# A hybrid attention block: one q/k tile set and one gate moved between fillers, memory weights split further ahead, a longer early output projection

## The chip, the cores and the metric

One core of a Trainium2 chip. The metric is the device time of one execution in microseconds (us). The engines meant below are TensorE (PE; its weight loads PEld overlap its matmuls), VectorE (DVE), ScalarE (ACT), GpSimd (POOL) and SyncE (SP, which issues every DMA of this kernel).

## The reference, cut to what matters

One layer for 512 tokens of width 1024: causal attention (8 heads of 64) and gated linear attention (4 heads) side by side on the same normed input, an output projection, cross-attention into 256 memory tokens, a squared-ReLU MLP, and norms between.

```python
h = rms_norm(x, norm_mix)
qa, ka, va, qg, kg, vg, glr, rg = split(h @ w_in)
o_a = moba_attention(qa, ka, va, rp_table)      # 512 tokens: 2 blocks of 256, both past and own visible: causal softmax
log_a = log_sigmoid(glr @ w_gate_up + b_gate) / 16
o_g = rms_norm(gla_chunked(qg, kg, vg, log_a), g_norm) * silu(rg)
x = x + concat([o_a, o_g]) @ w_out
m = rms_norm(mem, norm_mem)
kx, vx = split(m @ w_xkv)                        # needed by the cross-attention only
...
```

## The kernel before

All activations lie transposed (features on partitions). Every f32 weight tile of 128x1024 is loaded by SP into a staging buffer `wst` (5 of them) and split into two f16 halves in `whl` (10 buffers): ACT writes the high half (L114), DVE the low half (L115). Tiles are numbered in the order of use: `whl16` is the seventeenth. A product then takes three matmul passes for each slice of 128 inputs: high with high, high with low, low with high (L231 to L233 where the weights stand still, L246 to L248 where the activations do). A pass has 512 columns for the token activations and 256 for memory or for half of the tokens.

`W.get(key, look)` makes a tile and the `look` tiles after it at the point in the program where the tile is first used; `LOOK` is 3. PE executes its instructions in the order in which the program writes them. The order on ACT, DVE, POOL and SP is set by a list scheduler when the program is built, and each engine then works strictly through its own list. The rows of order below come from the built programs.

The stretch before the output projection has two parts. In the first, the linear attention (`Gla`, two pairs of heads, pr 0 and 1) is a chain of small matmuls and DVE/ACT steps; a queue of generators, `fill`, puts large products between its steps: `fill(n)` runs n steps of three passes (four to six of 256 columns for memory). The fillers are in order: `vg` (values of the linear attention), `qk_steps(0)`, `qk_steps(1)` (query and key tiles of the causal attention's head pairs: `qk0` and `qk4`, `qk1` and `qk5`), the memory's keys `xk0` to `xk7` and values `xv`, then `qk_steps(2)` (`qk2`, `qk6`) and the gates `rg_steps(0)`, `rg_steps(1)`. Before the first of them stands a transpose of the norm row `wx` on PE (L439).

In the second part, the causal attention works through four head pairs. Pair p needs the tiles of `qk_steps(p)`; `score(qt)` makes two PSUM banks of scores, DVE adds the bias and takes the maximum (L813), ACT the exponential (L817), both write the probabilities as two f16 halves `pq` (ACT L837, DVE L838), SP transposes them by DMA (L844) and `attn_out` (L856, bank `o0` to `o3`) multiplies by the values. Its result is split into `mix0` to `mix3`, one for each pair. The gates go into `mix4` to `mix7`, one for each head of the linear attention: `rg_steps(h)` evicts the product (DVE L415), and then ACT exp, DVE min (L538), ACT log, ACT exp, three DVE steps (L542 to L544), one product with the head's output (L545), and the split (ACT L277, DVE L278) follow one another. Fillers here are the values `va`, `qk_steps(3)` and the gates 2 and 3.

While the last pair's probabilities are on their way, `early_steps` begins the output projection in four PSUM banks `out0` to `out3`, on the slices of `mix` named there (slice k reads `mix`k); `residual_steps` adds the others after `o3`, in two halves of the tokens. The banks for scores, `o` and `out` are five (`sbank`), taken in turn. Everything behind the output projection, from the cross-attention's queries `xq` on, is untouched by the change.

Of the kernel before, what the change touches and what calls it, by code (L numbers as in the profile page):

```python
# [27 lines left out]
LOOK = 3  # L28
LOOK_MLP = 5


# [7 lines left out]
def hybrid_block_kernel(  # L39
# [163 lines left out]
    for n in range(8):  # L203
        W.add(("xv", n), w_xv[n])
    for n in (2, 6, 8, 9):
        W.add(("tt", n), w_tt[n])
    for n in range(4):
        W.add(("va", n), w_vv[n])
    for n in (3, 7, 10, 11):
        W.add(("tt", n), w_tt[n])  # L210
# [13 lines left out]

    def gemm_steps(ps, key, act, c0=0, c1=T, kts=range(8), start=True, stop=True, base=0, **kw):
        wt = W.get(key).rearrange("p s (k c) -> p s k c", k=8)
        kts = list(kts)
        for i, kt in enumerate(kts):
            a = act[base + kt]
            st, sp = start and i == 0, stop and i == len(kts) - 1  # L230
            PE.matmul(ps, wt[:, 0, kt, :], a[:, 0, c0:c1], start=st, stop=False, **kw)  # L231
            PE.matmul(ps, wt[:, 0, kt, :], a[:, 1, c0:c1], start=False, stop=False, **kw)  # L232
            PE.matmul(ps, wt[:, 1, kt, :], a[:, 0, c0:c1], start=False, stop=sp, **kw)  # L233
            yield
# [4 lines left out]

    def gemm_tok_steps(ps, keys, act, t0):  # L240
        ws = [W.get(k).rearrange("p s (k c) -> p s k c", k=2) for k in keys]
        for kt in range(8):
            w = ws[kt // 2]
            a = act[kt]
            st, sp = kt == 0, kt == 7
            PE.matmul(ps, a[:, 0, t0:t0 + P], w[:, 0, kt % 2, :], start=st, stop=False)  # L246
            PE.matmul(ps, a[:, 0, t0:t0 + P], w[:, 1, kt % 2, :], start=False, stop=False)
            PE.matmul(ps, a[:, 1, t0:t0 + P], w[:, 0, kt % 2, :], start=False, stop=sp)  # L248
            yield
# [186 lines left out]
    evict(glr, psg, 1.0)  # L436
    pw_ = sbank("wxt")
    for t in range(4):
        PE.transpose(pw_[:, t * P:t * P + P], wx[:, t * P:t * P + P], ident)  # L439
    DVE.tensor_scalar(wxt, pw_.rearrange("p (n t) -> p n t", t=P)[:, :, 0], SA * IX, None, op0=ALU.mult)  # L440

    def v3(t, s):
        return t.rearrange("p (n t) -> p n t", t=s)

    def vg_steps(t):
        ps = gbank(f"vg{t}")
        yield from gemm_tok_steps(ps, [("vg", j) for j in range(4)], act0, t * P)
        vg[t] = pg.tile([P, 512], F32, name=f"vgs{t}")
        ACT.activation(vg[t], ps, AF.Copy, scale=wxt[:, t:t + 1])
# [67 lines left out]
    def xk_steps(n):  # L517
        ps = gbank(f"xk{n}")[:, :M]
        for i, _ in enumerate(gemm_steps(ps, ("xk", n), actm, c1=M)):
            if i % 2:  # L520
                yield
        kf = pst.tile([P, M], F32, tag="yn", bufs=4, name=f"kf{n}")
        DVE.scalar_tensor_tensor(kf, ps, EM, wm, op0=ALU.mult, op1=ALU.mult)
        split(kx[n][:, 0, :], kx[n][:, 1, :], kf, 1.0)

    def xv_steps(c, t):
        ps = gbank(f"xv{c}{t}")
        yield from gemm_tok_steps(ps, [("xv", 4 * c + j) for j in range(4)], actm, t * P)
        cs = slice(c * 512, c * 512 + 512)
        split(vx[t][:, 0, cs], vx[t][:, 1, cs], ps, wmt[:, t:t + 1])  # L530
# [218 lines left out]
    fill.add(xk_steps(0), xk_steps(1), memrow_steps(), *[xk_steps(n) for n in range(2, 8)])  # L749
    fill.add(*[xv_steps(c, t) for c in range(2) for t in range(2)], qk_steps(2))  # L750
    gl = []
    for pr in range(2):
        fill(5)
        gl.append(Gla(pr))
    for pr in range(2):
        if pr == 1:
            load_bias(0)
        G = gl[pr]
        a = G.prep_fine()
        fill(20 if pr == 0 else 8)  # L760
        G.banks()
        G.small(0, a)
        for i, s in enumerate((8, 16)):
            a = G.prep_level(s)
            fill(5)
            G.small(128 + 128 * i, a)
# [12 lines left out]
        G.outp()  # L779
        fill(8)  # L780
        for hh in range(2):
            G.norm(hh)
            fill(6)
        if pr == 0:
            fill.add(rg_steps(0), rg_steps(1))
    fill.drain()
# [78 lines left out]
    def early_steps():  # L865
        for n in range(NPRE):
            early[n] = sbank(f"out{n}")
            yield from gemm_steps(early[n], ("out", n), mix, 0, T, (0, 1, 4, 5), stop=False, skip_group_check=True)

    def residual_steps(nm, act, hf, ssq):  # L870
        c0 = hf * HT
        for n in range(8):
            if nm == "out" and n < NPRE:
                ps = early[n][:, c0:c0 + HT]
                yield from gemm_steps(ps, (nm, n), act, c0, c0 + HT, (6, 7, 2, 3), start=False, skip_group_check=True)
            else:
# [14 lines left out]
    ssq = sums("out", *HALVES)  # L891
    fill.add(*[va_steps(t) for t in range(4)], qk_steps(3), rg_steps(2), rg_steps(3))
    pairs = {}
    for i in range(5):
        if i < 4:
            pairs[i] = Pair(i)
            if i < 3:
                load_bias(i + 1)
        if i == 3:
            fill.until(2)  # L900
        if i == 4:
# [3 lines left out]
        for g in range(4):  # L905
            if i < 4:
                pairs[i].score(3 - g)
                fill(5)
            elif g > 0:
                fill(4)  # L910
            if 1 <= i < 4 and g == 3:
                fill.until(3)
                attn_out(pairs.pop(i - 1))
        if i < 4:
            pairs[i].trans()
            fill(2)
    fill(4)
    attn_out(pairs.pop(3))
# [493 lines left out]
```

## Time and profile before

| | |
|---|---|
| median of 3 runs | 718.61 us (717.89 to 721.73) |
| profiled execution, its own time | 719.81 us |
| its span (first to last instruction) | 718.0 us |
| mean granted TensorE clock | 0.979 of full speed |
| PE busy | 681.6 us, 95% of the span |
| DVE busy / ACT busy | 553.9 us (77%) / 416.7 us (58%) |

The time is the whole execution as the device counts it, 1.8 us more than the span of the instructions in the same execution. Busy times are unions on one engine; the granted clock is 1.00 at 2.4 GHz and 0.50 at 1.2 GHz. Times within the trace are counted from the span's start.

### The profile page before, as it was taken

What the parts mean: (1) busy time and instruction counts of PE and PEld (TensorE: products, weight loads), DVE (VectorE), ACT (ScalarE), POOL (GpSimd) and SP (SyncE); (2) the same over time, 40 slices, a digit from 0 to 9 for tenths busy, and PEclk for the clock granted to TensorE, in tenths of its full rate; (3) what the DMA queues carried; (4) which work ended last, traced back from release to release, by engine and by line L of the source; (5) the groups of instructions that cost most, each with busy time, mean ns of one, the idle gap of its engine ahead of it and who ended that gap; (6) DMA issues with size and microseconds to landing.
All of it is one profiled execution on the core that took longest, in us unless ns stands there. A gap on an engine that the chain in (4) does not pass through costs nothing.

```text
span 718.0 us, 13472 instructions
## 1 busy us (share of the span) xinstructions
PE 681.6 (95%) x5376; PEld 472.7 (66%) x5376; DVE 553.9 (77%) x987; ACT 416.7 (58%) x800; POOL 72.0 (10%) x90
## 2 busy tenths in 40 slices
PE   8899997999995799999999999999999999999995
PEld 3344574454442378788888854458888866488884
DVE  6899448958888627847639899889888889999825
ACT  7755346846876617456536666555444766665533
POOL 4030010000000024200124100000000000003211
PEclk9999998999999799999999999999999999999998
DMA  8874005752486503325403332203333342314003
GB/s 307 278 259 133 1 1 174 270 174 76 113 236 216 116 21 119 118 60 169 113 16 109 128 102 75 88 31 119 118 119 118 120 164 70 117 50 144 16 1 118
DMA packets 57059, 85.68 MB, mean 119 GB/s; under 512 B 32123, under 2 KB 37540, under 8 KB 56996
## 3 DMA queue, kind: packets, MB, share of 16 engines
q1 hardware_dynamic: 56996, 84.82, 37.4%
q8 instruction: 42, 0.69, 0.4%
q14 instruction: 21, 0.17, 0.1%
HBM read 75.36 MB, written 3.68 MB: 110 GB/s over the span
## 4 chain that ended last, share of the span: by engine, by line
PE 57%; DVE 7%; ACT 2%; issue 2%; POOL 1%; DMA 1%; DVEq 0%; ACTq 0%; POOLq 0%
PE up L232 6%; PE up L233 6%; PE up L231 6%; PE a L1183 4%; PE a L1185 4%; PE a L1184 4%; DVE whl L115 2%; PE xq L231 2%; PE xq L233 2%; PE xq L232 2%; PE c L1184 2%; PE c L1185 2%; PE c L1183 2%; PE out L232 1%; PE out L231 1%
## 5 line engine op out<-in xcount | busy, mean ns | idle before, releaser
L115 DVE SCALAR_TENSOR_TENSOR whl<-wst,whl 128x1024 f16<-128x1024 f32 (+1 forms) x165 | 195.2, 1192 | 26.2 <-ACT whl L114 25.8
L114 ACT ACTIVATE whl<-wst 128x1024 f16<-128x1024 f32 (+1 forms) x165 | 165.6, 1013 | 43.0 <-PE a L1185 8.0
L231 PEld LDWEIGHTS <-whl 128*128 128x128 f16 x752 | 73.9, 98 | 43.3 <-ACT whl L114 5.5
L233 PEld LDWEIGHTS <-whl 128*128 128x128 f16 x752 | 73.9, 98 | 39.9 <-DVE whl L115 1.2
L232 PEld LDWEIGHTS <-whl 128*128 128x128 f16 x752 | 73.9, 98 | 36.2 <-issue 1.6
L232 PE MATMUL up<-act,whl 128*128 128x512 f16 (+1 forms) x224 | 78.1, 349 | 0.0
L233 PE MATMUL up<-act,whl 128*128 128x512 f16 (+1 forms) x224 | 78.1, 349 | 0.0
L231 PE MATMUL up<-act,whl 128*128 128x512 f16 (+1 forms) x224 | 78.1, 349 | 0.0
L1183 PE MATMUL a<-t,whl 128*128 128x256 f16 x192 | 52.3, 273 | 1.1 <-ACT v L1200 1.1
L1185 PE MATMUL a<-t,whl 128*128 128x256 f16 x192 | 52.3, 273 | 0.0
L1184 PE MATMUL a<-t,whl 128*128 128x256 f16 x192 | 52.3, 273 | 0.0
L1184 PEld LDWEIGHTS <-whl 128*128 128x128 f16 x456 | 44.6, 98 | 6.9 <-issue 1.5
L1183 PEld LDWEIGHTS <-whl 128*128 128x128 f16 x456 | 44.6, 98 | 5.2
L1185 PEld LDWEIGHTS <-whl 128*128 128x128 f16 x456 | 44.6, 98 | 5.0
L232 PE MATMUL xq<-act,whl 128*128 128x256 f16 x128 | 34.9, 273 | 0.2 <-DVE act L278 0.2
L233 PE MATMUL xo<-ox,whl 128*128 128x256 f16 x128 | 34.9, 273 | 0.0
L231 PE MATMUL xq<-act,whl 128*128 128x256 f16 x128 | 34.9, 273 | 0.0
L231 PE MATMUL xo<-ox,whl 128*128 128x256 f16 x128 | 34.9, 273 | 0.0
L232 PE MATMUL xo<-ox,whl 128*128 128x256 f16 x128 | 34.9, 273 | 0.0
L233 PE MATMUL xq<-act,whl 128*128 128x256 f16 x128 | 34.9, 273 | 0.0
L277 ACT ACTIVATE t<-hs 128x512 f16<-128x512 f32 x32 | 19.8, 624 | 23.9 <-DVE hs L1065 23.7
L232 PE MATMUL out<-mix,whl 128*128 128x256 f16 (+1 forms) x112 | 32.5, 290 | 0.2 <-DVE mix L278 0.2
(334 smaller groups left out, 1645.2 us busy)
## 6 DMA issues: line engine op xcount, KB each, us to landing
wst<-in_w_up SPq DMA_DIRECT2D x32, 512.0 KB, 3.8
wst<-in_w_down SPq DMA_DIRECT2D x32, 512.0 KB, 4.2
wst<-in_w_tt SPq DMA_DIRECT2D x12, 512.0 KB, 4.6
wst<-in_w_vv SPq DMA_DIRECT2D x8, 512.0 KB, 4.9
wst<-in_w_xk SPq DMA_DIRECT2D x8, 512.0 KB, 4.7
wst<-in_w_xv SPq DMA_DIRECT2D x8, 512.0 KB, 5.2
wst<-in_w_out SPq DMA_DIRECT2D x8, 512.0 KB, 3.7
wst<-in_w_xq SPq DMA_DIRECT2D x8, 512.0 KB, 3.6
```

What stands on the lines that cost most here:

```text
L114: ACT.activation(wt[:, 0, c], stg[:, c], AF.Copy, scale=SW)
L115: DVE.scalar_tensor_tensor(wt[:, 1, c], stg[:, c], SW, wt[:, 0, c], op0=ALU.mult, op1=ALU.subtract)
L231: PE.matmul(ps, wt[:, 0, kt, :], a[:, 0, c0:c1], start=st, stop=False, **kw)
L232: PE.matmul(ps, wt[:, 0, kt, :], a[:, 1, c0:c1], start=False, stop=False, **kw)
L233: PE.matmul(ps, wt[:, 1, kt, :], a[:, 0, c0:c1], start=False, stop=sp, **kw)
L277: ACT.activation(dst_h, src, AF.Copy, scale=scale)
L1183: PE.matmul(ps, w[:, 0, kt, :], b[:, 0, c], start=st, stop=False, skip_group_check=not start)
L1184: PE.matmul(ps, w[:, 0, kt, :], b[:, 1, c], start=False, stop=False, skip_group_check=not start)
L1185: PE.matmul(ps, w[:, 1, kt, :], b[:, 0, c], start=False, stop=sp, skip_group_check=not start)
```

## The change

The transpose of `wx` moves from ahead of the first filler to behind `Gla(0)`'s first matmul (`z0`); the `vg` tiles are made five ahead. The tiles of `xk` and `xv` are made six ahead instead of three. `qk_steps(2)` (48 passes) and `rg_steps(1)` (24 passes) leave the linear attention's fillers and become fillers of the causal attention; the numbers of filler steps are lowered in the first part and raised in the second, and the order of the weight tiles follows. The early output projection takes slices 6 and 7 too, that is, the gates of heads 2 and 3.

```diff
+LOOK_MEM = 6
...
-    for n in (2, 6, 8, 9):
-        W.add(("tt", n), w_tt[n])
+    W.add(("tt", 8), w_tt[8])
     for n in range(4):
         W.add(("va", n), w_vv[n])
-    for n in (3, 7, 10, 11):
+    for n in (2, 6, 3, 7, 9, 10, 11):
         W.add(("tt", n), w_tt[n])
...
-    pw_ = sbank("wxt")
-    for t in range(4):
-        PE.transpose(pw_[:, t * P:t * P + P], wx[:, t * P:t * P + P], ident)
-    DVE.tensor_scalar(wxt, pw_.rearrange("p (n t) -> p n t", t=P)[:, :, 0], SA * IX, None, op0=ALU.mult)
...
-        yield from gemm_tok_steps(ps, [("vg", j) for j in range(4)], act0, t * P)
+        yield from gemm_tok_steps(ps, [("vg", j) for j in range(4)], act0, t * P, 5)
...
-        for i, _ in enumerate(gemm_steps(ps, ("xk", n), actm, c1=M)):
+        for i, _ in enumerate(gemm_steps(ps, ("xk", n), actm, c1=M, look=LOOK_MEM)):
...
-    fill.add(*[xv_steps(c, t) for c in range(2) for t in range(2)], qk_steps(2))
+    fill.add(*[xv_steps(c, t) for c in range(2) for t in range(2)])
...
         gl.append(Gla(pr))
+        if pr == 0:
+            pw_ = sbank("wxt")
+            for t in range(4):
+                PE.transpose(pw_[:, t * P:t * P + P], wx[:, t * P:t * P + P], ident)
...
-        fill(20 if pr == 0 else 8)
+        fill(18 if pr == 0 else 6)
...
-            fill(5)
+            fill(4)
...
-        fill(8)
+        fill(6)
         for hh in range(2):
             G.norm(hh)
-            fill(6)
+            fill(4)
         if pr == 0:
-            fill.add(rg_steps(0), rg_steps(1))
+            fill.add(rg_steps(0))
...
-            yield from gemm_steps(early[n], ("out", n), mix, 0, T, (0, 1, 4, 5), stop=False, skip_group_check=True)
+            yield from gemm_steps(early[n], ("out", n), mix, 0, T, (0, 1, 4, 5, 6, 7), stop=False, skip_group_check=True)
...
-                yield from gemm_steps(ps, (nm, n), act, c0, c0 + HT, (6, 7, 2, 3), start=False, skip_group_check=True)
+                yield from gemm_steps(ps, (nm, n), act, c0, c0 + HT, (2, 3), start=False, skip_group_check=True)
...
-    fill.add(*[va_steps(t) for t in range(4)], qk_steps(3), rg_steps(2), rg_steps(3))
+    fill.add(*[va_steps(t) for t in range(4)], qk_steps(2), qk_steps(3), *[rg_steps(h) for h in (1, 2, 3)])
...
-        if i == 3:
-            fill.until(2)
+        if i in (2, 3):
+            fill.until({2: 4, 3: 3}[i])
...
-                fill(5)
+                fill(5 if i < 3 else 3)
...
-                fill.until(3)
+                fill.until(5)
...
-            fill(2)
-    fill(4)
+            fill(4)
+    fill(6)
```

Three places show how the lists move. The first is ACT's list in the first part, from the first step behind the norm sum `gss1` of pair 0 (`gv1`) on; `whl16` holds the tile of `xk3`, `whl19` that of `xk6`. Before:

```order
L712 ACTIVATE gv1_1166<-gss1_1164,eps_c_85 128x512
L284 ACTIVATE wg1_1169<-gv1_1166 128x512
L581 ACTIVATE qF_1_1230<-dF_1_1228 128x512
L285 ACTIVATE yg1_1168<-wg1_1169 128x512
L277 ACTIVATE kx4_96<-kf4_1188 128x256
L286 ACTIVATE wg1_1169<-yg1_1168 128x512
L582 ACTIVATE kF_1_1231<-dF_1_1228 128x512
L277 ACTIVATE kx5_97<-kf5_1236 128x256
L599 ACTIVATE qz8_1_1340<-d8_1_1338 128x32x8
L600 ACTIVATE kz8_1_1341<-d8_1_1338 128x32x8
L599 ACTIVATE qz16_1_1422<-d16_1_1420 128x16x16
L114 ACTIVATE whl19_1114<-wst19_1113 128x1024
```

and of the change, at the same place:

```order
L707 ACTIVATE gv1_1113<-gss1_1111,eps_c_85 128x512
L284 ACTIVATE wg1_1116<-gv1_1113 128x512
L285 ACTIVATE yg1_1115<-wg1_1116 128x512
L576 ACTIVATE qF_1_1165<-dF_1_1163 128x512
L286 ACTIVATE wg1_1116<-yg1_1115 128x512
L277 ACTIVATE kx2_94<-kf2_1135 128x256
L577 ACTIVATE kF_1_1166<-dF_1_1163 128x512
L594 ACTIVATE qz8_1_1253<-d8_1_1251 128x32x8
L595 ACTIVATE kz8_1_1254<-d8_1_1251 128x32x8
L594 ACTIVATE qz16_1_1329<-d16_1_1327 128x16x16
L115 ACTIVATE whl16_976<-wst16_975 128x1024
L115 ACTIVATE whl17_981<-wst17_980 128x1024
```

The first weight split behind this chain was that of `xk6`; now it is that of `xk3`, three tiles sooner in the order of use. On PE, 36 passes of `xk4` and `xk5` stood between `gss1` and `xk6`; now 12 of `xk2` stand between `gss1` and `xk3`.

The second place is PE's list in the early output projection, behind `out0`'s slices 0, 1 and 4. Before, slice 5 was the last, and `out1` followed:

```order
L231 MATMUL out0_2635<-mix5_110,whl41_2225 128x512
L232 LDWEIGHTS whl41_2225
L232 MATMUL out0_2635<-mix5_110,whl41_2225 128x512
L233 LDWEIGHTS whl41_2225
L233 MATMUL out0_2635<-mix5_110,whl41_2225 128x512
```

and of the change, behind the same slice 5:

```order
L231 MATMUL out0_2635<-mix6_111,whl41_2340 128x512
L232 LDWEIGHTS whl41_2340
L232 MATMUL out0_2635<-mix6_111,whl41_2340 128x512
L233 LDWEIGHTS whl41_2340
L233 MATMUL out0_2635<-mix6_111,whl41_2340 128x512
L231 LDWEIGHTS whl41_2340
L231 MATMUL out0_2635<-mix7_112,whl41_2340 128x512
L232 LDWEIGHTS whl41_2340
L232 MATMUL out0_2635<-mix7_112,whl41_2340 128x512
L233 LDWEIGHTS whl41_2340
L233 MATMUL out0_2635<-mix7_112,whl41_2340 128x512
```

The gates of heads 2 and 3 are now read by the first of the early banks, ahead of `out1`, `out2` and `o3`; before, they were read behind `o3`.

The third place is DVE's list where gate 3 ends (`rge3`, `rgu3`, `rgx3` are its buffers; `whl49` and `whl50` hold tiles of `xq`). Before, its last steps stood ahead of the splits of pair 3's probabilities:

```order
L543 SCALAR_TENSOR_TENSOR rgu3_2489<-rge3_2488,rgu3_2489 128x512
L814 TENSOR_SCALAR sm4_3_2501<-sm4_3_2501 128x2
L544 SCALAR_TENSOR_TENSOR rgx3_2487<-rgx3_2487,rgu3_2489 128x512
L820 RECIPROCAL sm4_3_2501<-sm4_3_2501 128x4
L545 TENSOR_TENSOR rgx3_2487<-rgx3_2487,mix7_112 128x512
L821 TENSOR_SCALAR sm4_3_2501<-sm4_3_2501 128x4
L278 SCALAR_TENSOR_TENSOR mix7_112<-rgx3_2487,mix7_112 128x512
L838 SCALAR_TENSOR_TENSOR pq3_0_2534<-p3_3_0_2510,sm4_3_2501,pq3_0_2534 128x3x128
```

and of the change all of pair 3's splits lie ahead of these rows:

```order
L540 TENSOR_TENSOR rgx2_2505<-rgx2_2505,mix6_111 128x512
L278 SCALAR_TENSOR_TENSOR mix2_107<-o2_2565,mix2_107 128x512
L415 SCALAR_TENSOR_TENSOR rgx3_2605<-rg3_2519,wx_124 128x512
L278 SCALAR_TENSOR_TENSOR mix6_111<-rgx2_2505,mix6_111 128x512
L116 SCALAR_TENSOR_TENSOR whl49_2849<-wst49_2848,whl49_2849 128x1024
L533 TENSOR_SCALAR rge3_2606<-rge3_2606 128x512
L116 SCALAR_TENSOR_TENSOR whl50_2883<-wst50_2882,whl50_2883 128x1024
L537 SCALAR_TENSOR_TENSOR rge3_2606<-rge3_2606,rgu3_2607 128x512
L538 SCALAR_TENSOR_TENSOR rgu3_2607<-rge3_2606,rgu3_2607 128x512
L539 SCALAR_TENSOR_TENSOR rgx3_2605<-rgx3_2605,rgu3_2607 128x512
L540 TENSOR_TENSOR rgx3_2605<-rgx3_2605,mix7_112 128x512
L278 SCALAR_TENSOR_TENSOR mix7_112<-rgx3_2605,mix7_112 128x512
```

Gate 3 has moved behind pair 3's probabilities and behind two weight splits. (The change's line numbers differ by a few from those of before.)

## Rows read from the trace of the kernel before

**Rows 1.** The page: busy us of each engine, share of the span, instructions.

```profile
PE 681.6 (95%) x5376; PEld 472.7 (66%) x5376; DVE 553.9 (77%) x987; ACT 416.7 (58%) x800; POOL 72.0 (10%) x90
```

**Rows 2.** Windows: stretch, length, busy by engine, granted clock, DMA share, GB/s.

```profile
31.45:41.28 9.83, 7.07 (x23) 2.77 (x24) 8.30 (x12) 8.11 (x16) 3.09 (x2) 0.83 0.91 330
...
106.70:120.30 13.60, 7.62 (x49) 5.52 (x48) 11.28 (x19) 7.25 (x11) 0.00 (x0) 0.75 0.35 116
...
224.87:256.65 31.78, 19.66 (x119) 10.19 (x118) 19.96 (x58) 17.37 (x45) 0.00 (x0) 0.79 0.51 125
256.65:287.43 30.78, 30.78 (x280) 27.50 (x280) 17.14 (x33) 15.38 (x31) 12.84 (x14) 1.00 0.23 70
287.43:718.00 430.57, 418.15 (x3356) 326.95 (x3353) 343.40 (x575) 241.49 (x460) 38.51 (x39) 0.99 0.30 95
```

**Rows 3.** Waits of PE: who for whom, us, times, longest.

```profile
PE s L809 <- DVE mix L278: 8.1, 1, 8.1
...
PE o L856 <- DMA pT<-pq: 2.3, 1, 2.3
...
PE s L809 <- DVE sm L813: 1.5, 2, 0.8
...
PE xk L233 <- DVE whl L115: 0.7, 1, 0.7
```

**Rows 4.** Timeline of PE: start, us, instructions, idle before and its releaser.

```profile
34.21 0.66 PE L439 MATMUL wxt<-ident,wx 128*128 128x128 f32 x4 [2.76 <-DVE wx L289]
...
40.43 1.02 PE L557 MATMUL z<-glr,csb 128*128 128x512 f32 x2
...
101.75 1.02 PE L710 MATMUL gss<-gsq,ones 128*128 128x512 f32 x2
...
111.95 0.39 PE L231 MATMUL xk<-mix,whl 128*128 128x256 f16 x1 [5.24 <-ACT whl L114]
...
129.74 0.38 PE L246 MATMUL xv<-whl,mix 128*128 128x512 f16 x1
...
132.76 0.38 PE L248 MATMUL xv<-whl,mix 128*128 128x512 f16 x1
...
171.08 0.82 PE L809 MATMUL s<-qks,qks 64*128 64x512 f16 x6
...
210.48 0.66 PE L809 MATMUL s<-qks,qks 64*128 64x384 f16 x6
...
253.39 1.82 PE L856 MATMUL o<-pT,vas 128*64 128x512 f16 x24
```

**Rows 5.** Timeline of DVE, the same columns.

```profile
34.08 1.22 DVE L115 SCALAR_TENSOR_TENSOR whl<-wst,whl 128x1024 f16<-128x1024 f32 x1
35.21 2.47 DVE L415 SCALAR_TENSOR_TENSOR gqk<-g,wx 128x512 f32<-128x512 f32 x4
37.60 0.68 DVE L415 SCALAR_TENSOR_TENSOR glr<-glr,wx 128x512 f32<-128x512 f32 x1
...
38.27 0.54 DVE L726 COPY bvec<-bv 8x384 f32<-8x384 f32 x1
...
240.87 0.69 DVE L278 SCALAR_TENSOR_TENSOR mix<-rgx,mix 128x512 f16<-128x512 f32 x1 [0.69 <-ACT mix L277]
241.48 2.73 DVE L838 SCALAR_TENSOR_TENSOR pq<-p,sm,pq 128x384 f16<-128x384 f32 x6
...
245.13 1.41 DVE L838 SCALAR_TENSOR_TENSOR pq<-p,sm,pq 128x256 f16<-128x256 f32 x4
```

**Rows 6.** Timeline of ACT, the same columns.

```profile
110.86 3.88 ACT L114 ACTIVATE whl<-wst 128x1024 f16<-128x1024 f32 x4
```

**Rows 7.** Windows, from pair 2's second score to gate 3's split.

```profile
211.14:241.56 30.42, 18.54 (x124) 8.97 (x125) 24.63 (x75) 21.99 (x56) 0.00 (x0) 0.81 0.74 201
```

**Rows 8.** Timeline of SP's DMA issues: x for the residual, pair 2's transposes.

```profile
217.00 5.24 SPq L888 DMA_DIRECT2D xr<-in_x_t  x8
...
231.48 5.27 SPq L844 DMA_TRANSPOSE pT<-pq  x2
```

More of the change, by code (lines that the diff above doesn't have):

```diff
@@ L222, in hybrid_block_kernel, with gemm_steps @@
             W.add_unit(m, j)
-    def gemm_steps(ps, key, act, c0=0, c1=T, kts=range(8), start=True, stop=True, base=0, **kw):
-        wt = W.get(key).rearrange("p s (k c) -> p s k c", k=8)
+    def gemm_steps(ps, key, act, c0=0, c1=T, kts=range(8), start=True, stop=True, base=0, look=LOOK, **kw):
+        wt = W.get(key, look).rearrange("p s (k c) -> p s k c", k=8)
         kts = list(kts)
@@ L238, in gemm, with gemm_tok_steps @@
             pass
-    def gemm_tok_steps(ps, keys, act, t0):
-        ws = [W.get(k).rearrange("p s (k c) -> p s k c", k=2) for k in keys]
+    def gemm_tok_steps(ps, keys, act, t0, look=LOOK):
+        ws = [W.get(k, look).rearrange("p s (k c) -> p s k c", k=2) for k in keys]
         for kt in range(8):
@@ L527, in xv_steps @@
         ps = gbank(f"xv{c}{t}")
-        yield from gemm_tok_steps(ps, [("xv", 4 * c + j) for j in range(4)], actm, t * P)
+        yield from gemm_tok_steps(ps, [("xv", 4 * c + j) for j in range(4)], actm, t * P, LOOK_MEM)
         cs = slice(c * 512, c * 512 + 512)
@@ L754, in hybrid_block_kernel @@
         gl.append(Gla(pr))
+        if pr == 0:
+            pw_ = sbank("wxt")
+            for t in range(4):
+                PE.transpose(pw_[:, t * P:t * P + P], wx[:, t * P:t * P + P], ident)
+            DVE.tensor_scalar(wxt, pw_.rearrange("p (n t) -> p n t", t=P)[:, :, 0], SA * IX, None, op0=ALU.mult)
     for pr in range(2):
```

## The prediction

> **What bounds the kernel now.** I read the page first: TensorE is busy for 681.6 of 718.0 us, so a gain must come out of its idle time or its slow clock [rows 1]. The chain of waits and the windows by stage say where those lie. From 287.43 us on, where `xq` starts, TensorE is busy 418.15 of 430.57 us and nothing is changed there [rows 2]. The loss ahead of that has three places [rows 2 to 4].
>
> - The start: TensorE waits 2.76 us for the norm row before `wxt`, and `z` starts at 40.43; 31.45 to 41.28 runs at 0.83.
> - The memory's keys: 106.70 to 120.30 takes 13.60 us for 48 passes. At full speed a pass of 256 columns takes 30.78 / 280 = 0.110 us; I use 0.114, so 5.5 us would do. The rest is a wait of 5.24 us for ACT's split `whl19`, one of 0.7, and about 2 us of the slower clock (0.75).
> - The attention's tail: 224.87 to 256.65 has 19.66 us busy in 31.78, with waits of 8.1 (a score bank held until DVE has split a `mix`), 2.3 and 1.5 us.
>
> So the sum follows TensorE to the start of `xq`, and asks of every wait who releases it.
>
> **The start.** In the new lists `vg` runs right behind the gate's small product, and `z0` still reads `glr`, which DVE evicts. That eviction starts at 37.60 and `bvec` behind it at 38.27 [rows 5]. One weight split moves from ahead of it to behind it: 35.21 - 34.08 = 1.13 us less. `bvec` moves ahead: its 0.54 row, of which some 0.47 show start to start, more. `glr` then ends near 38.27 - 1.13 + 0.47 = 37.6, `z0` starts near 37.7 instead of 40.43, and the `wxt` transposes behind it take about 0.33 at full clock: 2.4 us saved. The other end: the wait is still about 2 us, and if the clock falls as before, the 9.83 us with 7.07 of work [rows 2] give up to 1.7 back: 0.7 saved. I take 2.4.
>
> **The memory.** Six tiles ahead would remove the 5.24 us if the split could be done earlier. But ACT works through its list in order: after `gss1` (101.75) come pair 0's norm and pair 1's preparation, and only at 110.86 the four splits of 0.97 us each [rows 4, 6]. In the new list the first split behind the same chain is `xk3`'s instead of `xk6`'s. So TensorE's release stays where it is, about 9.1 us behind `gss1`'s start, while its cover shrinks from 36 passes to 12: 24 x 0.114 = 2.7 us more wait, 7.9 instead of 5.24. One split of a key (a few tenths of a us) has left that stretch of ACT's list, so the lower end is 2.4. Afterwards a split comes every 1.13 us and a tile lasts 24 x 0.114 = 2.7 us; the 0.7 wait may go, I leave it. The DMAs are covered: their share there is 0.35 [rows 2].
>
> **Where the attention starts.** The 48 passes of `qk2` and `qk6` and the 24 of gate 1 are now behind it. A pass of 512 columns: 129.74 to 132.76 holds 14 of them, 0.216 us each [rows 4]; 72 x 0.216 = 15.5. The first score moves from 171.08 to 171.08 - 15.5 - 2.4 + 2.7 = 155.9.
>
> **To pair 2's second score.** Before, that ends at 211.14, 40.06 us after the first score, without a wait. Now 15 more passes stand before it (3.2 us), and pair 2's first score must wait for `qk6`, whose last product is just ahead of it. Eviction and split of `qk6` and the weight splits that ACT and DVE have ahead of them, 1.0 and 1.13, with 0.6 to split, are covered by three passes: 2.2 us (1 to 3). So 45.5 us, and the score ends at 201.4.
>
> **To gate 3's split.** From here DVE and ACT set the pace. Before, `mix7` was finished 30.42 us after this score, with DVE busy 24.63 of them [rows 7]. In the new list DVE has more ahead of `mix7`: gate 1's seven steps, each 0.60 start to start as the four `gqk` (2.47 us) show [rows 5], 4.2; the eviction and split of one more tile, 1.2; two weight splits, 2.3; pair 3's probabilities, 2.73 + 1.41 = 4.1; `o2`'s split, 0.6. Together 12.4, so 42.8 us, and `mix7` comes at 155.9 + 45.5 + 42.8 = 244.2, against 241.56 before. Lower end: DVE never waits, 24.63 + 12.4 = 37.0, `mix7` at 238.4. Upper end: it waits in the same proportion, 37.0 x 30.42 / 24.63 = 45.7, 247.1. I take the middle, since the added steps fill some of the 5.8 us but need ACT between them.
>
> On these starts there is a rule against the change. The four `gqk` start 0.60 apart although one lasts 0.68, and the weight splits 1.13 apart against 1.22 [rows 5]. The Trainium skill, "VectorE: DVE Perf Modes", section "The DRAIN you can't avoid", says that the next DVE operation doesn't start until the pipe is empty. By that rule each of some 18 added steps costs about 0.08 us more, 1.4 in all, and the result would be 1.4 us later than mine. The rows say otherwise for instructions that wait for nothing, and the measurement decides.
>
> **TensorE until then and after.** The work left between the second score and `out0`'s gate slices is about 31 us (30 passes of `qk3` and `qk7` and 72 of gates 22.0, six groups of scores at 0.3 to 0.8 together 3, `o1` and `o2` 1.82 each, 12 passes of `out0` 2.6), so TensorE gets there near 232.3 and waits, first for `mix6`, then for `mix7`, 12 us in all. These waits replace the 8.1 and 2.3 of before. After `mix7` follow 2 passes of `out0` and 36 of `out1` and `out2`, 38 x 0.216 = 8.2, and some 2.1 us of clock, as the old tail lost. Then `o3`. From `o3` to `xq` it was 287.43 - 253.39 = 34.0. Slices 6 and 7 of four banks in two halves, 48 passes x 0.110 = 5.3, are gone; `out3`, which stood ahead of `o3`, comes behind it with 18 passes, 3.9. That gives 32.6. So `xq` starts at `mix7` + 42.9 = 287.1 instead of 287.43: **0.3 us saved**.
>
> The transfers don't enter this. SP's eight loads of x (217.00, 5.24 us of issue) stand, in the new list, behind gate 3's last product (near 230) and ahead of pair 3's transposes, which in pair 2 began at 231.48 [rows 8]. Those would land some 8 us behind the loads, near 243; `o3` starts near 254.5. That cover of 11 us hides them; without it the loads would cost up to 5.2.
>
> The profiled execution took 719.81 us, so 719.5 after. The median of the runs is 1.2 us below that execution: **718.3 us**. Half a per cent, 3.6 us, is about what a measurement of this kernel can tell from no change. The break-even is `mix7` at 244.5; faster by 3.6 needs it by 240.9 (a stretch of 39.5 us in place of 42.8), slower by 3.6 from 248.1 on (46.7).
>
> **The rivals.**
> *Fewer waits on DVE.* The fillers lie more evenly now and DVE is the only limit of the stretch: `mix7` at 238.4, `xq` at 281.3, 6.1 us faster, 712.4. For it: five of DVE's 30.42 us were waits that more work can fill. Against it: each gate is a chain through ACT and DVE, and gate 3 now stands last. 0.17.
> *The fillers fill all of the attention's idle time.* TensorE would never wait behind the first scores: `o3` at 232.3 + 9.1 = 241.4, `xq` at 274.0, 13.4 us, 705.2. It needs `mix7` within 31.6 us, less than the 37.0 of work that DVE has by my count. 0.03. The Trainium skill, "Perfetto Trace Analysis", section "Identifying the Most-Contended Engine", says that interleaving regimes with different contended engines may improve performance; this would be that case.
> *The look ahead does remove the memory's wait.* Then the attention starts 7.9 us sooner, and with some 2 us of clock and the 0.7 regained about 11 us are saved: 707.4. Against it: the split's place in ACT's list. 0.04.
> *Slower: gate 3's chain crosses between ACT and DVE behind pair 3's probabilities.* DVE's last rows alternate between gate 3 and two weight splits, with ACT's exponentials and logarithms between. If DVE's waits in the stretch are 12 us instead of 5.8, it is 49 us, `mix7` comes at 250.4, and the kernel takes 724.2. It decides from 46.7 us on, or from 9.7 of waits. For it: the upper proportion already gives 45.7; against it: before, the same gate chain ran within 5.8 us of waits. 0.18.
> That the start saves 0.7 only costs 1.7 and leaves the time within the half per cent: 720.0.
>
> **How the numbers follow.** My forecast, no change to be measured, has 0.58, and its own range is 714.7 to 722.2. Faster: 0.17 + 0.03 + 0.04 = 0.24. Slower: 0.18. The range of 711.8 to 724.0 takes in DVE without waits and most of the slower case, and leaves out the two large gains, some of the slow case, and what I have overlooked.
>
> **What the profile after would show.** Right: `z0` at 37 to 38 behind a wait of about 2 us; one wait of some 8 us on ACT's `whl` at `xk3`; the first score near 156; a wait of about 2 us on `qks` at pair 2's first score; `out0` waiting for `mix6` and `mix7` until about 244, and no long wait for a score bank or for `pT`; `xq` near 287. Wrong: if the wait at `xk3` is short, the attention starts by 150 and the whole gains; if `mix7` is done by 239 or behind 248, DVE's count is wrong, and its busy time between the second score and `mix7` (37 expected) tells whether by work or by waits; if `o3` waits for `pT`, SP's order was the miss.

## The result and the profile after

The changed kernel takes 728.3 us (median of 4 runs, 726.67 to 728.91); the kernel before took 718.25 beside it (717.41 to 721.73). The ratio is 1.0127 (95% interval 1.009 to 1.0164; the two medians alone would give 1.014): slower, where no change was forecast. The profiled execution took 728.34 us, 8.5 more than that of before. The rows below, of its page, show that TensorE's work is about that of before [rows 1]: 24 instructions fewer, since 48 passes of 256 columns became 24 of 512. The 8.6 us of longer span are waits (4.9 us of idle time) and slow clock (3.7 us more busy).

```profile
span 726.6 us, 13422 instructions
PE 685.3 (94%) x5352; PEld 469.6 (65%) x5352; DVE 553.3 (76%) x987; ACT 416.6 (57%) x800; POOL 75.1 (10%) x90
```

The waits of TensorE, who for whom, us, times, longest (against [rows 3]):

```profile
PE out L231 <- ACT mix L277: 8.3, 2, 5.4
PE xk L231 <- ACT whl L115: 7.6, 1, 7.6
PE xq L232 <- DVE act L278: 3.3, 5, 1.1
PE psL L609 <- DVE kF L579: 1.6, 1, 1.6
...
PE z L552 <- DVE glr L415: 1.4, 1, 1.4
...
PE s L809 <- ACT qks L277: 1.0, 1, 1.0
PE s L809 <- DVE qks L278: 1.0, 1, 1.0
...
PE xq L231 <- ACT act L277: 0.9, 2, 0.5
PE out L232 <- DVE mix L278: 0.8, 1, 0.8
```

The long waits for a score bank, for `pT` and for `wx` are gone. The gates' (`out`), the memory's (`xk`) and the two small ones (`z`, `qks`) were forecast. Not forecast are those of `psL` (the small products of the linear attention) and of `xq`. The timeline of TensorE gives the places (against [rows 4]):

```profile
37.35 1.13 PE L552 MATMUL z<-glr,csb 128*128 128x512 f32 x2 [1.40 <-DVE glr L415]
...
56.31 0.76 PE L609 MATMUL psL<-qF,kF 64*32 64x32 f32 x64 [1.64 <-DVE kF L579]
...
105.99 0.40 PE L231 MATMUL xk<-mix,whl 128*128 128x256 f16 x1 [7.63 <-ACT whl L115]
...
158.92 0.82 PE L809 MATMUL s<-qks,qks 64*128 64x512 f16 x6
...
205.45 0.66 PE L809 MATMUL s<-qks,qks 64*128 64x384 f16 x6
...
248.40 0.59 PE L231 MATMUL out<-mix,whl 128*128 128x512 f16 x1 [5.44 <-ACT mix L277]
...
258.76 0.62 PE L856 MATMUL o<-pT,vas 128*64 128x512 f16 x3
...
291.21 0.27 PE L231 MATMUL xq<-act,whl 128*128 128x256 f16 x1
292.36 0.27 PE L232 MATMUL xq<-act,whl 128*128 128x256 f16 x1 [0.89 <-DVE act L278]
```

DVE's timeline has the end of gate 3's split:

```profile
248.38 0.69 DVE L278 SCALAR_TENSOR_TENSOR mix<-rgx,mix 128x512 f16<-128x512 f32 x1 [0.69 <-ACT mix L277]
```

Step by step, in us:

| | before | forecast | after |
|---|---|---|---|
| `z0` starts | 40.43 | 37.7 | 37.35 |
| wait of `xk` on ACT | 5.24 | 7.9 | 7.63 |
| first score | 171.08 | 155.9 | 158.9 |
| from there to pair 2's second score's end | 40.06 | 45.5 | 47.2 |
| from there to the end of `mix7`'s split | 30.42 | 42.8 | 43.0 |
| `o3` starts | 253.39 | 254.5 | 258.76 |
| from `o3` to `xq` | 34.04 | 32.6 | 32.45 |
| from `xq` to the end of the span | 430.57 | 430.57 | 435.4 |

Against the 719.5 us that the prediction had for this execution, it is 8.8 us late: `xq` starts 4.1 us later than forecast, and 4.8 us more go behind it. The windows by stage (length, busy by engine, clock) show where; first those of the changed kernel:

```profile
206.10:248.86 42.76, 33.69 (x204) 14.52 (x203) 37.73 (x95) 30.20 (x69) 0.00 (x0) 0.92 0.60 173
...
291.20:403.90 112.70, 108.50 (x966) 95.33 (x965) 74.90 (x164) 59.11 (x142) 18.65 (x17) 0.98 0.34 93
403.90:726.60 322.70, 312.20 (x2392) 232.51 (x2389) 271.62 (x421) 185.06 (x325) 20.50 (x24) 0.99 0.29 94
```

and the last two stretches in the kernel before:

```profile
287.43:395.10 107.67, 106.12 (x967) 94.46 (x965) 71.88 (x155) 56.45 (x136) 18.04 (x16) 1.00 0.35 98
395.10:718.00 322.90, 312.03 (x2392) 232.49 (x2389) 271.52 (x421) 185.04 (x325) 20.46 (x24) 0.99 0.29 94
```

DVE's 37.73 us busy of the 42.76 (a window that ends 0.2 us short of `mix7`'s split) is near what was counted (37.0 of 42.8). The loss behind `xq` lies wholly in the cross-attention: 112.70 against 107.67 us up to the MLP's first product `up`, and no more behind it. Of these 5.0 us, 2.6 are more idle time (4.20 against 1.55) and 2.4 are longer busy time (108.50 against 106.12): behind the waits TensorE's clock fell, and from 299.8 to 302.8 a pass of 256 columns starts every 0.21 us instead of every 0.11.

### The profile page after: what moved, and what is told of

Read it like the earlier page. It is cut to its first block, busy times and chain, and to the rows that moved or that the text cites. A ratio compares the mean times of both kernels' runs of the same rounds, so it can differ in the third digit from the quotient of the medians.

```text
span 726.6 us, 13422 instructions
## 1 busy us (share of the span) xinstructions
PE 685.3 (94%) x5352; PEld 469.6 (65%) x5352; DVE 553.3 (76%) x987; ACT 416.6 (57%) x800; POOL 75.1 (10%) x90
## 4 chain that ended last, share of the span: by engine, by line
PE 59%; DVE 8%; ACT 3%; issue 1%; POOL 1%; DVEq 0%; ACTq 0%; POOLq 0%
PE up L232 6%; PE up L231 6%; PE up L233 6%; PE a L1183 4%; PE a L1185 4%; PE a L1184 4%; PE xq L232 2%; PE xq L233 2%; PE xq L231 2%; PE c L1184 2%; PE c L1183 2%; PE c L1185 2%; DVE whl L116 2%; PE out L232 1%; PE out L233 1%
## 5 line engine op out<-in xcount | busy, mean ns | idle before, releaser
L232 PE MATMUL xq<-act,whl 128*128 128x256 f16 x128 | 35.5, 277 | 3.3 <-DVE act L278 3.3
L231 PE MATMUL xq<-act,whl 128*128 128x256 f16 x128 | 35.5, 277 | 0.9 <-ACT act L277 0.9
L233 PE MATMUL xq<-act,whl 128*128 128x256 f16 x128 | 35.5, 277 | 0.0
```

## The experiments

All ratios are to the kernel before on the same chip, over 4 to 11 runs of each variant and 11 to 17 of the kernel before; times within a run are those of one profiled execution.

### What each part does by itself

**Six early slices alone**: the kernel before with this edit, and nothing else.

```diff
-            yield from gemm_steps(early[n], ("out", n), mix, 0, T, (0, 1, 4, 5), ...)
+            yield from gemm_steps(early[n], ("out", n), mix, 0, T, (0, 1, 4, 5, 6, 7), ...)
-                yield from gemm_steps(ps, (nm, n), act, c0, c0 + HT, (6, 7, 2, 3), ...)
+                yield from gemm_steps(ps, (nm, n), act, c0, c0 + HT, (2, 3), ...)
```

> The kernel before with one part of the change alone: the early output projection takes slices 6 and 7 (six slices early, two behind o3). Theory A (the early gates cost twice, once in front of o3 and once behind the second half of the residual, where the norm for xq loses its cover): here the gates are on time, since mix7 was finished at 241.6 and out0 reads it near 245, so only the second cost shows: xq starts at 286 to 288, then waits for its input some 4 us in all, and the kernel takes 722 to 724. Rival B (only the lateness of the gates costs, the shorter residual nothing): 717 to 719.

1.0045 (1.0028 to 1.0062), 723.4 us. `xq` starts at 287.1, as before, and then waits:

```profile
PE xq L232 <- DVE act L278: 3.0, 4, 1.0
...
PE xq L231 <- ACT act L277: 0.5, 1, 0.5
```

From `xq` on it takes 435.7 us instead of 430.6. Theory A, not B: with gates on time the six slices still cost 3 us (by the medians).

**The changed kernel with this edit undone** (the same lines the other way; four early slices, and the first two steps of the residual, `out0`'s slices 6 and 7, still stand ahead of `o3`):

> The changed kernel with slices 6 and 7 put back behind o3. Theory A: TensorE reaches out0 at 235, runs 48 passes (10.4 us) without a wait, o3 starts near 246, mix7 (249) is waited for 1 to 2 us at most, xq starts near 281 to 283 and runs without waits: 711 to 715, faster than the kernel before. Rival B (the gates that were moved are late wherever they are read): the 5.4 us wait for mix7 stands behind o3 and the time stays at 722 or more.

0.9929 (0.991 to 0.9949), 715.3 us. `o3` starts at 248.10 instead of 258.76, `xq` at 283.3, and the rest is back at 430.6. Between the profiled executions lie 12.7 us: 1.5 up to the first score (157.4 and 158.9), 9.2 from there to `o3`, 4.8 behind `xq`, less 2.8 between `o3` and `xq`. The 1.5 are not the edit's: up to there the two programs have the same lists on every engine. The edit that looked like a rearrangement of equal work turned a gain into a loss. Rival B is out: read later, the gates are waited for 3.5 us in all instead of 9.1 (1 to 2 were forecast).

**The fillers alone**: the kernel before with the moved tile set, gate and filler numbers; start, look ahead and early slices as before. Against the run above:

```diff
-LOOK_MEM = 6
+LOOK_MEM = 3
...
     evict(glr, psg, 1.0)
+    pw_ = sbank("wxt")
+    for t in range(4):
+        PE.transpose(pw_[:, t * P:t * P + P], wx[:, t * P:t * P + P], ident)
...
-        yield from gemm_tok_steps(ps, [("vg", j) for j in range(4)], act0, t * P, 5)
+        yield from gemm_tok_steps(ps, [("vg", j) for j in range(4)], act0, t * P)
```

> The kernel before with the moved tile set and gate and the numbers of filler steps alone (start, look ahead and early slices as before). Theory A: what the start gained was given back at the first small products of pair 0, and the look ahead only moved the memory's wait, so this stands within 1.5 us of the run with slices 6 and 7 put back: 712 to 716. Rival: start and look ahead are worth 3 us or more together, and this is 3 us or more slower than that run.

0.9895 (0.988 to 0.991), 712.5 us, the best of the parts, and better than the run before it by more than the 1.5 us allowed between them in spans (712.0 against 713.9). The first score comes at 154.5, against 157.4 in that run. So start and look ahead together cost some 2 us. The wait at `xk` is the row below; that of the run with start and look ahead is 7.6, as in the changed kernel:

```profile
PE xk L231 <- ACT whl L115: 4.5, 1, 4.5
```

**The start alone**: the kernel before with the transposes of `wx` behind `z0` and `vg` five ahead.

```diff
         gl.append(Gla(pr))
+        if pr == 0:
+            pw_ = sbank("wxt")
...
-        yield from gemm_tok_steps(ps, [("vg", j) for j in range(4)], act0, t * P)
+        yield from gemm_tok_steps(ps, [("vg", j) for j in range(4)], act0, t * P, 5)
```

> The kernel before with the moved transpose of wx and the vg tiles five ahead alone. Prediction's step: z0 starts 2.4 us or more sooner, and all of it is kept: 715 to 716. Theory A: z0 starts some 3 us sooner, but psL or a later step of pair 0's chain, or the wait at xk, takes it back: 717.5 to 719.

0.9991 (0.9979 to 1.0003), 719.5 us: the prediction's step (715 to 716) is out. `z0` starts at 37.2, 3.2 us sooner, and the first score at 171.4, 0.3 us later. A new wait of `psL` takes 1.9 us of it; the waits at `xk` are 5.5 together, against 5.9, and the rest lies in no single wait:

```profile
PE psL L609 <- DVE kz L597: 1.9, 1, 1.9
```

**Gate 1 left in the linear attention**: the fillers alone, but only `qk2` and `qk6` moved.

```diff
-            fill.add(rg_steps(0))
+            fill.add(rg_steps(0), rg_steps(1))
...
-    fill.add(*[va_steps(t) for t in range(4)], qk_steps(2), qk_steps(3), *[rg_steps(h) for h in (1, 2, 3)])
+    fill.add(*[va_steps(t) for t in range(4)], qk_steps(2), qk_steps(3), *[rg_steps(h) for h in (2, 3)])
```

> The run with the fillers alone, but gate 1 stays in the linear attention; only the tile set qk2, qk6 moves (48 of 72 passes). The attention of before waited 8.1, 2.3 and 1.5 us. If the tile set fills most of that and gate 1's 24 passes (5.2 us) find little left, the ratio is within 0.002 of the 0.9895 of both; if the gate pays as well in proportion, it is 0.992 to 0.995.

0.9888 (0.9862 to 0.9915), 712.3 us, no different from both. In the profiled executions the attention from first score to `xq` takes 120.2 us with the tile set and 126.5 with the gate too: 24 passes, 5.2 us of work, took 6.3 us there. The tile set (10.4 us of work) took 3.9 more than the 116.3 of before [rows 2, 4]. It used up the idle time, and the gate found none.

### Where the time behind xq goes

**Slices 6 and 7 early for the first half of the tokens only**, in the changed kernel:

```diff
-            yield from gemm_steps(early[n], ("out", n), mix, 0, T, (0, 1, 4, 5, 6, 7), ...)
+            yield from gemm_steps(early[n], ("out", n), mix, 0, T, (0, 1, 4, 5), ...)
+            yield from gemm_steps(early[n][:, :HT], ("out", n), mix, 0, HT, (6, 7), start=False, ...)
-                yield from gemm_steps(ps, (nm, n), act, c0, c0 + HT, (2, 3), ...)
+                yield from gemm_steps(ps, (nm, n), act, c0, c0 + HT, (6, 7, 2, 3) if hf else (2, 3), ...)
```

> The changed kernel with slices 6 and 7 early for the first half of the tokens only; the second half adds them behind o3 as before. Theory A: the second half's 24 passes again cover the norm, the waits of xq (4.2 us) fall below 0.5 and the stretch from xq's start to the end is 4 to 5 us shorter than in the changed kernel (435.4); the wait of out0 for the gates stays at 8 us or more, so the ratio to before is 1.003 to 1.008. Rival: xq's waits come from the late gates or from elsewhere, and the stretch stays at 434 or more, the ratio at 1.011 or more.

1.0052 (1.0031 to 1.0072), 722.9 us. The gates are waited for as long as ever, and behind `xq` everything is as before:

```profile
PE out L231 <- ACT mix L277: 8.7, 2, 5.9
PE ssqout L332 <- POOL accout L327: 1.4, 1, 1.4
...
PE xq L232 <- DVE act L278: 0.2, 1, 0.2
```

Theory A, as forecast. The norm of the first half runs while TensorE works on the second half of the residual; 24 passes of that half (2.6 us) had been taken away. In the kernel before and in this run `xq` starts 13.9 us behind the norm's sum `ssqout` (273.57 before); in the changed kernel it is 11.4, by the first row and the start of `xq` above. But the same edit also reordered DVE's list. The second row is the split of the first `act` tile in the changed kernel, the third that of the kernel before:

```profile
279.80 0.60 PE L332 MATMUL ssqout<-accout,ones 128*128 128x256 f32 x2
```

```profile
291.90 0.41 DVE L278 SCALAR_TENSOR_TENSOR act<-ynout,act 128x256 f16<-128x256 f32 x1
```

```profile
283.11 1.08 DVE L278 SCALAR_TENSOR_TENSOR act<-ynout,act 128x256 f16<-128x256 f32 x3
```

It comes 12.1 us behind `ssqout` there and 9.5 before (9.5 in this run too). So this run shows that the 24 passes are the cause, and leaves open how much goes by the shorter cover and how much by the order of the lists. The next two runs ask that.

**Own buffers for the squares**, four instead of the two shared ones, for the residual's second half of the changed kernel. Behind it stands this piece of the changed kernel's ACT timeline, where the norm's square root `yout` lies behind a square that waits for POOL:

```profile
281.31 0.40 ACT L316 ACTIVATE sqout<-xr 128x256 f32<-128x256 f32 x1
283.25 0.42 ACT L316 ACTIVATE sqout<-xr 128x256 f32<-128x256 f32 x1 [1.54 <-POOL accout L327]
283.57 0.40 ACT L285 ACTIVATE yout<-wout 128x256 f32<-128x256 f32 x1
```

```diff
+                if self.name in own:
+                    sq = own[self.name].tile([P, self.n], F32, tag="sqo", bufs=4, ...)
...
+    own[f"out{HT}"] = s4.enter_context(tc.tile_pool(name="psq", bufs=4, reuse_waits="tile"))
```

> The changed kernel with four buffers of their own for the squares of the residual's second half, so that ACT needn't wait there for POOL's sums; the order of ACT's list stays. Theory E, the norm for xq is late because its square root on ACT (yout) stands behind a square that waits 1.5 us for POOL: yout comes 1.5 us sooner behind ssqout, xq's waits fall from 4.2 to about 2.5, the ratio to 1.010 to 1.011. Rival F, only the lost cover counts (24 passes, 2.6 us) and the rest is DVE's list: xq's waits stay at 4 us, the ratio at 1.012 to 1.013.

1.0109 (1.0086 to 1.0131), 727.5 us; this doesn't part E from F. ACT now shows:

```profile
280.19 0.40 ACT L285 ACTIVATE yout<-wout 128x256 f32<-128x256 f32 x1
```

`yout` comes 2.1 us behind `ssqout` (278.1) instead of 3.8 (279.8), but DVE's list puts weight splits (at 283.37 and 285.38) around the two steps that use it, and `xq` still waits 3.3 us.

**The residual's second half in the order `out4` to `out7`, `out0` to `out3`**, in the changed kernel:

```diff
-        for n in range(8):
+        for n in (4, 5, 6, 7, 0, 1, 2, 3) if nm == "out" and hf else range(8):
```

> The changed kernel with the residual's second half in the order out4 to out7, out0 to out3. The passes between ssqout and xq are as few as in the changed kernel, but in ACT's list the norm's three steps now stand ahead of the squares and of all weight splits but one. Theory E (the norm chain is held up in the lists): the first act tile is ready 8 to 9.5 us behind ssqout instead of 12, xq's waits fall below 1 us, 3 to 4 us come back, ratio 1.007 to 1.009. Rival F (lost cover only): xq's waits stay at 3 us or more, ratio 1.011 or more.

1.009 (1.0067 to 1.0112), 726.0 us. DVE splits the first `act` tile 6 us behind `ssqout` instead of 12, and `xq`'s wait falls to 1.0, but the other half's norm waits in its place:

```profile
PE ssqout L332 <- POOL accout L327: 3.0, 1, 3.0
...
PE xq L232 <- DVE act L278: 1.0, 1, 1.0
```

4.0 us in all, nearly as in the changed kernel; 434.5 us from `xq` on. The ratio alone would pass for E, but of the 3.1 us between the profiled spans 2.2 lie ahead of `xq`. E was right on the order and wrong on what it is worth: of the 4.8 us behind `xq`, 0.9 came back. In this run and the changed kernel, with 24 passes fewer, one of the two norms is waited for, whichever comes first.

### What sets the memory's wait

**The changed kernel with four early slices and the start as before**: the fillers alone, but with `LOOK_MEM` 6.

> The changed kernel with slices 6 and 7 behind o3 and the start as before (the wx transpose ahead of the first filler, vg three ahead); the memory's tiles stay six ahead. It stands beside two runs: slices 6 and 7 put back (ratio 0.9929 to before, wait of 7.6 us at the first xk split behind gss1) and the fillers alone (0.9895, 4.5 us). Theory C, the move of the wx transpose makes the memory's wait longer, since in its lists the splits of xk3 to xk5 have moved behind pair 0's norm chain: here they stand ahead of it again, the wait is about 4.5 us and the ratio 0.988 to 0.991. Rival D, the six tiles ahead do it: the wait stays near 7.6 us and the ratio near 0.993.

0.9915 (0.989 to 0.9941), 713.8 us; the wait at `xk` is 4.5 us again. The ratio is just above C's 0.988 to 0.991, but the wait decides for theory C: with these fillers the moved transpose makes it 7.6, and the six tiles ahead change nothing that shows. SP's timeline says how. Before (L731 spreads the bias vector over 1.5 MB of DRAM; six loads of `xk` stand ahead of it, so the first behind it is that of `xk6`):

```profile
39.23 1.07 SPq L113 DMA_DIRECT2D wst<-in_w_xk  x2
...
40.74 0.76 SPq L731 DMA_DIRECT2D bscr<-bscr  x1
48.96 12.61 SPq L113 DMA_DIRECT2D wst<-in_w_xk  x2
```

and in the changed kernel, where three stand ahead of it and the first behind it is that of `xk3`:

```profile
34.73 0.80 SPq L114 DMA_DIRECT2D wst<-in_w_xk  x2
38.92 0.77 SPq L726 DMA_DIRECT2D bscr<-bscr  x1
...
39.78 23.25 SPq L114 DMA_DIRECT2D wst<-in_w_xk  x5
```

With the transposes gone from before `bvec`, the bias goes out earlier, ahead of three more loads. In the programs of before, of the change and of the fillers alone, the first weight split behind pair 0's norm chain is that of the first tile loaded behind this DMA. The start alone fits less well: there too `xk3` is the first load behind the DMA, but its split stands between the norms of pair 0's two heads, and the waits at `xk` came to 5.5 us, not more than before. So the 7.6 us need the moved transpose and the new fillers together.

**That DMA issued by POOL instead of SP**, in the kernel before:

```diff
-    nc.sync.dma_start(
+    nc.gpsimd.dma_start(
         bass.AP(tensor=bscr.tensor, ...),
         bass.AP(tensor=bscr1.tensor, ...),
     )
```

> The kernel before with one DMA moved: the spreading of the bias vector in DRAM (bscr from bscr, 1.5 MB) is issued by POOL instead of SP. In every run so far the first weight split that lies behind pair 0's norm chain is that of the first tile whose load stands behind this DMA on SP: xk6 before (wait 5.2 us), xk3 with the moved wx transpose (7.6 us), xk6 again with the start undone (4.5 us). Theory G, the place of this DMA on SP sets the memory's wait: here the splits lie ahead of the chain, the waits at xk fall below 1 us, the first score moves from 171.1 to 164 to 166, ratio 0.990 to 0.994. Rival H, ACT and DVE have no room and the chain of pair 0 or 1 waits instead: first score at 169 or later, ratio 0.997 or more.

0.9932 (0.991 to 0.9954), 715.3 us. No wait at `xk` is left; the first score starts at 164.5, 6.6 us sooner, and `xq` at 281.0, 6.4 sooner. Theory G.

**The same with the fillers alone:**

> The run with the fillers alone (0.9895) and the same DMA on POOL. Theory G: the waits of 4.5 and 0.7 us at xk go, with some 1 to 2 us of slow clock, first score at 148 to 150 instead of 154.5, ratio 0.981 to 0.984. Rival H: 0.987 or more.

0.9869 (0.9841 to 0.9897), 709.9 us, the lowest ratio here, though its interval overlaps that of the fillers alone. The wait at `xk` is gone, but the first score comes only 1.3 us sooner (153.2). The splits, now early, stand in DVE's list ahead of `kz`; the timelines of DVE and then TensorE:

```profile
58.65 4.60 DVE L116 SCALAR_TENSOR_TENSOR whl<-wst,whl 128x1024 f16<-128x1024 f32 x4
63.17 0.41 DVE L602 TENSOR_TENSOR kz<-kz,gqk 128x256 f32<-128x256 f32 x1
```

```profile
63.73 0.88 PE L614 MATMUL psL<-qz,kz 64*32 64x32 f32 x64 [4.98 <-DVE kz L602]
```

So the place in the list is G's, and most of its gain goes as H said.

**The same with start and six tiles ahead** (four early slices):

> The changed kernel with slices 6 and 7 behind o3 and the same DMA on POOL; the start and the six tiles ahead stay. Theory G with C (the moved transpose cost the memory's wait through SP's order only): the wait of 7.6 us goes too, first score at 147 to 150 instead of 157.4, ratio 0.979 to 0.984, within 1.5 us of the fillers alone with this DMA. Rival D: the wait stays at 4 us or more, ratio 0.988 or more.

0.9917 (0.9887 to 0.9947), 713.9 us, first score at 157.6: a miss. The 7.6 us at `xk` are gone, as C and G have it, but `psL` waits 8.2 us for `kz` and 2.8 for `kF`, and nothing is gained. `kz` stands behind four weight splits in this list too; they take 6.74 us here, 4.60 in the run above.

**The two last runs with the old numbers of filler steps in the linear attention** (20 and 8, 5, 8, 6):

```diff
-        fill(18 if pr == 0 else 6)
+        fill(20 if pr == 0 else 8)
...
-            fill(4)
+            fill(5)
...
-        fill(6)
+        fill(8)
...
-            fill(4)
+            fill(6)
```

First the fillers alone with the DMA on POOL,

> The run with the fillers and the bias DMA on POOL (ratio 0.9869, first score 153.2), with the numbers of filler steps in the linear attention as before (20 and 8, 5, 8, 6 where the change has 18 and 6, 4, 6, 4). There the memory's wait was gone, but TensorE waited 1.2 and 5.0 us at psL of pair 0, for kF and for kz behind four weight splits on DVE (4.6 us), where the kernel before with the same DMA waited 1.9 us. Theory J, the lowered numbers take pair 0's cover away: psL waits 2 us or less in all, first score at 148 to 150, ratio 0.980 to 0.984. Rival K, DVE's chain sets the pace and the fillers used here are missing later: psL or another step of pair 1 waits as much, first score at 152.5 or later, ratio 0.986 or more.

0.9886 (0.9858 to 0.9913), 711.5 us. `psL` waits 1.5 us and the first score starts at 150.6, 2.5 us sooner: so far J. But `xq` starts at 278.6, against 277.6 with the lowered numbers; from first score to `xq` it now takes 128.0 us instead of 124.4. In the result K (the two ratios are not apart), though not by pair 1: the attention gave it back. Then the same with start and six tiles ahead:

> The changed kernel with slices 6 and 7 behind o3, the bias DMA on POOL (0.9917, first score 157.6, psL waits 8.2 and 2.8 us) and the old numbers of filler steps. Theory J: psL's waits fall by 3 us or more, first score at 152 to 154, ratio 0.985 to 0.988. If the moved start pays once its cover is back, it comes within 0.002 of the run without it; if the start is what makes DVE's chain late (e of pair 0 behind the memory's squares on ACT), it stays 2 us or more behind that run.

0.9919 (0.9887 to 0.995), 713.3 us. The wait for `kz` stays at 7.6 us. By the medians the run is 1.8 us behind the last one, but the two intervals overlap, and the run also has six tiles ahead: that the start itself costs time here isn't shown. What it can run into is in ACT's timeline of the changed kernel,

```profile
44.22 0.63 ACT L490 ACTIVATE sqm<-memf 128x512 f32<-128x512 f32 x1 [3.32 <-POOL accm L491]
44.76 1.04 ACT L115 ACTIVATE whl<-wst 128x1024 f16<-128x1024 f32 x1
45.70 0.67 ACT L556 ACTIVATE e<-z,gsb 128x512 f32<-128x512 f32 x1
```

beside the kernel before:

```profile
42.27 0.69 ACT L561 ACTIVATE e<-z,gsb 128x512 f32<-128x512 f32 x1 [0.54 <-DVE g L559]
```

`z0` is ready 3 us sooner, but `e`, the next step, stands behind a square of the memory that waits for POOL, and starts 3.4 us later than before. That belongs to this execution and not to the lists alone: in four other runs whose lists are the same up to the early output projection (four early slices, first half only, own buffers, other order) `e` starts at 42.6, 44.9, 42.5 and 41.9, and with the start alone at 41.3. What differs is POOL's pace (last section).

## Why the prediction was wrong

**"From 287.43 us on nothing is changed there"** is the step that failed: it took 435.4 us and not 430.57, 4.8 of the 8.8 us by which the forecast was missed. The instructions are the same, but `xq` reads the norm of the first half, and the prediction itself took its cover away: it booked the 24 passes of the second half as saved between `o3` and `xq` and didn't ask what ran beside them. The half-only run puts them back and has all of it back (430.6). The term had been right in size (32.6 forecast, 32.45 measured); its other side was missing. In the changed kernel that side was 2.6 us of idle time, as much as the 24 passes take, and the slow clock behind the waits.

**The start, "2.4 us saved"**, was right to `z0` and lost behind it: in the profiled execution at the next step of the chain, ACT's `e`, and at `psL`; with slow clock and smaller waits the first score came 3.0 us later than forecast. In the four other runs with the same lists it came at 157.4 to 158.5, so 1.5 to 2.6 us late whatever `e` did. Alone, the start is worth nothing (0.9991), though `e` starts 1.0 us sooner there.

**The memory's wait** was right in size (7.9 forecast, 7.63) and only half explained. That the new lists put `xk3` behind the norm chain was read off; that, with the new fillers, the moved transpose did it, through a DMA on SP, wasn't. That the six tiles ahead remove nothing was right.

**To pair 2's second score**, 47.2 instead of 45.5: the wait for `qks` was 2.0 us as forecast, but the slow clock (0.96 for the stretch, 1.00 before) was left out.

**The DVE chain to gate 3** was right: 43.0 us, 42.8 forecast. That the two agree to 0.2 us is partly luck, since 0.7 us more work and 0.8 less waiting offset each other. So the slow rival (gate 3's chain with 12 us of waits) isn't what happened: DVE waited 5 us. What the forecast didn't draw from it is that the early slices make TensorE wait for that chain at all. It set the gain of the fillers against this wait and came out at nothing. Measured apart, the fillers give 1.0% and the six slices take 2.0% from the changed kernel.

On starts: in the changed kernel DVE steps over 128x512 that don't read one another begin 0.60 us apart as before (240.00, 240.61, 241.20), each lasting 0.69. The rule of the Trainium skill, "VectorE: DVE Perf Modes", section "The DRAIN you can't avoid", is not what these rows show; the section itself leaves room for instructions that aren't held. Gate 3's last steps, each of which reads the one before, begin 0.73 apart (245.54, 246.27, 246.99). The busy time, 37.73 us where 37.0 was counted and the rule would give 1.4 more, doesn't decide.

The 48 moved passes paid (0.9888), the 24 behind them no more. The regime rule of the Trainium skill, "Perfetto Trace Analysis" (it stands in the section "Optimization Strategy" there), agrees with the first of these numbers; it doesn't say where the gain ends.

Three of the prediction's rivals are 0.1 to 0.3 us off the times that their own terms give (712.5, 707.7 and 724.5); nothing hangs on that.

Still open is how the attention gave back the 2.5 us that the old filler numbers won, where the start's gain goes when `e` isn't late, and how much of the loss behind `xq` is cover and how much the order of DVE's list.

## What to carry to other kernels

Work that is moved away from a place can be a loss there if something ran beneath it: look for the reader behind the stretch that becomes shorter, even where that reader's own code is untouched. Ask of every stall removed at the head of a chain for the next instruction on the other engines' lists, since the 3 us that TensorE gained at `z0` were worth nothing here, with ACT's next step at best 1.0 us sooner. Where a scheduler orders the lists, a small edit can move a DMA on a shared queue and with it the place of work that has nothing to do with it; compare the queue's order as well.

## What was not expected of the hardware

The same operation of POOL over 128x512 took very different times. Its timeline in the changed kernel, and DVE's beside it,

```profile
37.61 3.31 POOL L487 TENSOR_SCALAR accm<-accm 128x512 f32<-128x512 f32 x1 [22.66 <-ACT accm L486]
```

```profile
37.23 2.33 DVE L116 SCALAR_TENSOR_TENSOR whl<-wst,whl 128x1024 f16<-128x1024 f32 x2
39.49 0.73 DVE L554 TENSOR_SCALAR g<-z,gsb 128x512 f32<-128x512 f32 x1
```

and in the kernel before:

```profile
36.56 1.49 POOL L492 TENSOR_SCALAR accm<-accm 128x512 f32<-128x512 f32 x1 [22.04 <-ACT accm L491]
```

It took 3.31 against 1.49 us; the three sums behind it took 5.88 together, and 1.27 to 1.60 each before. Through two shared buffers this reached ACT and the chain behind it.

Of the eight traces with the moved start four have 1.49 us (start alone, four early slices, own buffers, other order) and four have 3.31 to 4.03 (the changed kernel, first half only, and the two with the DMA on POOL). In the long ones DVE's two weight splits begin before POOL's step or at most 0.33 us behind its start, and the step ends 1.42 to 1.43 us after the DVE step behind these splits has begun. In the short ones POOL starts 0.44 us or more ahead of the splits. So the step seems to stand still while DVE splits, and which of the two comes first differs between executions of the same lists. No run tests this, and a profile's spans on POOL are rough.

The 1.5 MB DMA from DRAM to DRAM took 1.3 us of POOL's time when POOL issued it and landed 11 to 13 us later; TensorE waited nowhere for it.
